# Attention softmax of a decoder layer: diagonal steps of 384 columns, mask and maximum in one instruction, key sums as products with a column of ones

## The chip, the cores and the metric

The kernel runs on one NeuronCore of a Trainium2 chip. The metric is the time of one execution in device microseconds; before the change the median of three runs is 2763.43 us (2759.95 to 2764.75). Engines are named as in the profile: PE is TensorE (PEld its weight loads), DVE is VectorE, ACT is ScalarE, POOL is GpSimd, SP is SyncE.

## The reference

One layer of a decoder over 2048 tokens of width 1024, all in float32. A normalised input is projected into three groups of columns: latent attention (8 heads, 96 wide for scores and 64 for values, causal), a spatial gating branch and a short convolution. Their outputs are normalised, joined and projected back, and a SwiGLU channel mixer with 2816 hidden columns follows. The change lies in the attention alone:

```
sc = (q_nope @ k_nope.T + q_rope @ k_rope.T) * scale
sc = where(kpos <= qpos, sc, lowest)
p  = softmax(sc, axis=-1)
out = p @ v
```

## The kernel before, in words

Products that need float32 accuracy are made of three products of float32r parts: each operand is split into a high part (ACT copies it) and a low part (DVE or POOL subtracts), and high x high, high x low and low x high are added in PSUM (`mm3_steps`, L204 to L206). A few small products take float32 operands as they are: `fold` (L518) is one.

The work goes in stages: input projections (to about 330 us), then attention woven with the rest of gating and the convolution (`weave`, L966; called from L1284 on), with the output projection of the first half, and with the channel mixer of the first half; from about 1800 us on the second half runs without attention. `attention` is a generator that yields an estimated cost after each piece, and the weaving takes so much of the other work for it. A scheduler of the build then sets each engine's order.

Attention has 64 units: 8 heads x 8 query blocks of 256 queries (`qp` 0 to 7; query blocks 0 to 3 of all heads come first). A unit has `qp + 1` steps, each over 256 keys, two blocks of 128 (`u`). The last step, `j2 == qp`, is the diagonal one: its second key block is seen by the second half of the queries alone. In all there are 288 steps, 64 of them diagonal.

For a unit, in the order in which it is planned:
- `row_max` (L420 to L440): for each half `e` of the queries, one product with queries on the partitions gives up to 512 scores in a PSUM bank `s`; DVE adds the mask `causal` to the last 128 columns of the last block (L435) and takes the maximum of each block (L436); with more than one block a last reduction (L439) joins them, negated, in column 96 of a tile `nmw`.
- `put_rows` (L442): PE transposes the two `nmw` tiles (128 x 97) into `mrow`, and ACT copies row 96 to the query tile as its 97th row, so that the scores come out with the maximum subtracted.
- `scores` (L451): per step two `mm3` into `sT` (keys on the partitions, 2 x 256 query columns). On a diagonal step DVE adds `causT` to two squares of 128 columns, the third square of `p` is set to zero by DVE (L467), and ACT takes the exponential in two pieces (L468, L469); otherwise one piece of 512 (L471). ACT copies `p` to `ph`, POOL (or DVE) makes `pl`. DVE adds every `p` to a running sum `acc` (L481, L484).
- `values` (L487), three steps later: per key block two products of the values with `ph` and `pl` into the PSUM bank `o`, of which there is one. At the unit's end DVE adds the halves of `acc` into `tot` (L503), ACT copies `o` to `os` (L505).
- `finish` (L510): PE transposes `tot` (two products, L516) and multiplies `os` by `fold` (two float32 products, L518), all into the bank `of`; DVE reduces the transposed `tot` to one sum per query (L520), takes the reciprocal and scales the output (L526).

The PSUM banks of `s`, `mrow` and `of` come from two tags of one bank each ("nx"), which the transposes of the output projection use too.

Of the kernel before, what the change touches and what calls it, by code (L numbers as in the profile page):

```python
# [11 lines left out]
F32 = mybir.dt.float32  # L12
# [3 lines left out]
AF = mybir.ActivationFunctionType  # L16
ALU = mybir.AluOpType
AX = mybir.AxisListType

P = 128  # L20
# [5 lines left out]
GT = 256  # L26
GELU_C = 0.044715
PB = 3
LAG = 3
TB = 3  # L30
# [6 lines left out]
NMB = 4  # L37
# [37 lines left out]
NEG = -1e30  # L75
# [9 lines left out]
def trunk(  # L85
# [6 lines left out]
    nc = tc.nc  # L92
# [7 lines left out]
    const = ctx.enter_context(tc.tile_pool(name="const", bufs=1))  # L100
# [12 lines left out]
    ident = const.tile([P, P], F32, name="ident")  # L113
# [4 lines left out]
    fold = const.tile([P, 64], F32, name="fold")  # L118
    for i in range(2):
        half = slice(64 * i, 64 * i + 64)  # L120
        nc.vector.tensor_copy(fold[half], ident[half, half])

    causal = const.tile([P, P], F32, name="causal")
    make_causal_mask(nc, causal, mask_val=NEG)
    causT = const.tile([P, P], F32, name="causT")
    nc.gpsimd.memset(causT, 0.0)
    nc.gpsimd.affine_select(out=causT, in_=causT, compare_op=ALU.is_ge, fill=NEG, base=0,
                            pattern=[[1, P]], channel_multiplier=-1)
    nmw = [const.tile([P, 97], F32, name=f"nmw{i}") for i in range(2 * NMB)]
    for t in nmw:  # L130
        nc.gpsimd.memset(t, 0.0)

    gp = const.tile([P, KD], F32, name="gp")

# [27 lines left out]
    def rows(t):  # L162
        return slice(t * P, (t + 1) * P)
# [215 lines left out]
    def attention(pools):  # L379
# [38 lines left out]
        mxs = {}  # L418

        def row_max(n, e, b):  # L420

            part, hd, qp = units[n]
            nk = (2 * qp + e + 1) * P
            nb = (nk + 511) // 512
            nm = nmw[(2 * n + e) % (2 * NMB)]
            if b == 0:
                mxs[n, e] = sp.tile([P, 4], F32, name="mx", bufs=4)
            mx = mxs[n, e]
            w = min(512, nk - 512 * b)
            wm = (w + GT - 1) // GT * GT  # L430
            s = bank("nx", "s")
            nc.tensor.matmul(s[:, :wm], qts[n][0:96, 0, rows(e)], kts[part, hd, b][0:96, 0:wm // GT, 0, :],  # L432
                             start=True, stop=True)
            if b == nb - 1:
                nc.vector.tensor_tensor(s[:, w - P:w], s[:, w - P:w], causal, op=ALU.add)  # L435
            nc.vector.tensor_reduce(mx[:, b:b + 1] if nb > 1 else nm[:, 96:97], s[:, :w],  # L436
                                    axis=AX.X, op=ALU.max, negate=nb == 1)
            if nb > 1 and b == nb - 1:
                nc.vector.tensor_reduce(nm[:, 96:97], mx[:, :nb], axis=AX.X, op=ALU.max, negate=True)  # L439
            return 0.7  # L440

        def put_rows(n):  # L442

            qt = qts[n]
            mrow = bank("nx", "mrow")
            for e in range(2):
                nc.tensor.transpose(mrow[0:97, rows(e)], nmw[(2 * n + e) % (2 * NMB)], ident)
            nc.scalar.activation(qt[96:97, 0, :], mrow[96:97, 0:GT], AF.Copy)
            return 0.4

        def scores(n, j2, st):  # L451
            part, hd, qp = units[n]
            qt = qts[n]
            s = bank("s", "sT")
            for u in range(2):
                j = 2 * j2 + u
                g, keys = j % 4 // 2, rows(j % 2)
                kt = kts[part, hd, j // 4]
                seen = slice(P if j2 == qp and u else 0, GT)
                mm3(s[:, u * 256 + seen.start:u * 256 + 256],  # L460
                    lambda k: kt[:, g, 0, keys], lambda k: kt[:, g, 1, keys],
                    lambda k: qt[:, 0, seen], lambda k: qt[:, 1, seen], 1)
            p = sp.tile([P, 512], F32, name="p", bufs=PB)
            if j2 == qp:
                for cs in (slice(0, P), slice(3 * P, 4 * P)):
                    nc.vector.tensor_tensor(s[:, cs], s[:, cs], causT, op=ALU.add)
                nc.vector.memset(p[:, 2 * P:3 * P], 0.0)  # L467
                nc.scalar.activation(p[:, 0:2 * P], s[:, 0:2 * P], AF.Exp)  # L468
                nc.scalar.activation(p[:, 3 * P:], s[:, 3 * P:], AF.Exp)  # L469
            else:  # L470
                nc.scalar.activation(p, s, AF.Exp)  # L471
            ph_ = sp.tile([P, 512], F32R, name="ph", bufs=PB)
            nc.scalar.activation(ph_, p, AF.Copy)  # L473
            pl_ = sp.tile([P, 512], F32R, name="pl", bufs=PB)
            eng = nc.vector if (n * 7 + j2) % 8 < lo_share[0] else nc.gpsimd
            eng.tensor_tensor(pl_, p, ph_.bitcast(F32), op=ALU.subtract)  # L476
            if j2 == 0:
                st["acc"] = p
            elif j2 == 1:
                acc = sp.tile([P, 512], F32, name="acc")  # L480
                nc.vector.tensor_tensor(acc, st["acc"], p, op=ALU.add)  # L481
                st["acc"] = acc
            else:
                nc.vector.tensor_tensor(st["acc"], st["acc"], p, op=ALU.add)  # L484
            return ph_, pl_

        def values(n, j2, pp, st):  # L487
            part, hd, qp = units[n]
            if j2 == 0:
                st["o"] = bank("o", "o")  # L490
            o = st["o"]
            for u in range(2):
                j = 2 * j2 + u
                at = P if j2 == qp and u else 0
                for i in range(2):
                    nc.tensor.matmul(o[:, at:256], vts[part, hd, j // 8][:, j % 8, :],  # L496
                                     pp[i][:, u * 256 + at:u * 256 + 256],
                                     start=j == 0 and i == 0, stop=j2 == qp and u == 1 and i == 1)
            if j2 < qp:
                return  # L500
            acc = st["acc"]
            tot = sp.tile([P, 256], F32, name="tot", bufs=TB)
            nc.vector.tensor_tensor(tot, acc[:, 0:256], acc[:, 256:512], op=ALU.add)  # L503
            os = sp.tile([P, 256], F32, name="os", bufs=TB)
            nc.scalar.activation(os, o[:, 0:256], AF.Copy)  # L505
            done[n] = tot, os

        done, yas = {}, {}

        def finish(n):  # L510

            _, hd, qp = units[n]
            of = bank("nx", "of")
            tot, os = done.pop(n)
# [11 lines left out]
            nc.vector.tensor_tensor(ya[:, :, 64 * (hd % 2):64 * (hd % 2) + 64],  # L526
                                    of[:, 256:384].rearrange("p (e d) -> p e d", e=2),
                                    rs[:, 2:4].unsqueeze(2).broadcast_to([P, 2, 64]), op=ALU.mult)
# [10 lines left out]
        for n in reversed(range(NU)):  # L539
            part, hd, qp = units[n]  # L540
# [47 lines left out]
        sp = pools[0]  # L588
# [5 lines left out]
        k = 0  # L594
        for n in range(NU):
            st = {}
            qp = units[n][2]
# [16 lines left out]
    with ExitStack() as ph:  # L614
# [3 lines left out]
        sp = ph.enter_context(tc.tile_pool(name="a_s", bufs=2, reuse_waits="tile"))  # L618
# [761 lines left out]
```

## Time and profile before

| | |
|---|---|
| median of three runs | 2763.43 us (2759.95 to 2764.75) |
| the profiled execution | 2758.1 us, of which the span (first to last instruction) is 2756.2 us |
| PE busy | 2673.9 us, 97% of the span, 14076 instructions |
| PEld busy | 2295.6 us, 83% |
| DVE busy | 1593.9 us, 58% |
| ACT busy | 1030.3 us, 37% |
| POOL busy | 751.9 us, 27% |
| mean granted TensorE clock | 0.979 |

The time of the profiled execution is that of the run in which the trace was taken; the span is what its rows cover. Busy times of one engine are unions over its instructions; matmuls are pipelined, so the duration of one is longer than its distance from the next, and it is the distances that add up to the time.

### The profile page before, as it was taken

What the parts mean: (1) busy time and instruction counts of PE and PEld (TensorE: products, weight loads), DVE (VectorE), ACT (ScalarE), POOL (GpSimd) and SP (SyncE); (2) the same over time, 40 slices, a digit from 0 to 9 for tenths busy, and PEclk for the clock granted to TensorE, in tenths of its full rate; (3) what the DMA queues carried; (4) which work ended last, traced back from release to release, by engine and by line L of the source; (5) the groups of instructions that cost most, each with busy time, mean ns of one, the idle gap of its engine ahead of it and who ended that gap; (6) DMA issues with size and microseconds to landing.
All of it is one profiled execution on the core that took longest, in us unless ns stands there. A gap on an engine that the chain in (4) does not pass through costs nothing. (4 is left out here: it accounts for less than half of the span.)

```text
span 2756.2 us, 37469 instructions
## 1 busy us (share of the span) xinstructions
PE 2673.9 (97%) x14076; PEld 2295.6 (83%) x14076; DVE 1593.9 (58%) x2805; ACT 1030.3 (37%) x1921; POOL 751.9 (27%) x835
## 2 busy tenths in 40 slices
PE   8999989998998999999999999999999999999998
PEld 7999878888787888888888888877878888888886
DVE  6555585657777666757687676755443333333335
ACT  6434353444455434444444444433531111111112
POOL 1222335765343332333343223313100000000004
PEclk9999988998999999999999999999999999999999
DMA  8755765454245333333252322254541111111113
GB/s 299 224 183 175 236 192 160 138 162 145 84 145 188 94 103 92 95 92 104 87 177 90 113 71 86 66 182 138 181 147 46 46 46 46 46 46 46 47 39 122
DMA packets 268945, 329.42 MB, mean 120 GB/s; under 512 B 17646, under 2 KB 198300, under 8 KB 264092
## 3 DMA queue, kind: packets, MB, share of 16 engines
q1 hardware_dynamic: 261244, 293.46, 34.0%
q0 software_dynamic: 5184, 29.36, 3.2%
q10 hardware_dynamic: 2336, 4.20, 0.4%
q8 instruction: 111, 1.82, 0.3%
q14 instruction: 70, 0.57, 0.1%
HBM read 238.56 MB, written 86.25 MB: 118 GB/s over the span
## 5 line engine op out<-in xcount | busy, mean ns | idle before, releaser
L476 POOL TENSOR_TENSOR pl<-p,ph 128x512 fp32r<-128x512 f32 x240 | 346.0, 1447 | 642.6 <-ACT ph L473 470.8
L1165 DVE TENSOR_TENSOR acc<-pd,acc 128x512 f32<-128x512 f32 x304 | 206.1, 688 | 225.1 <-PE pd L206 224.4
L204 PE MATMUL gu<-h2T,wgh 128*128 128x512 f32 x704 | 277.4, 394 | 2.6 <-ACT h2T L166 2.6
L205 PE MATMUL gu<-h2T,wgh 128*128 128x512 f32 x704 | 276.9, 393 | 0.0
L206 PE MATMUL gu<-h2T,wgl 128*128 128x512 f32 x704 | 276.8, 393 | 0.0
L204 PE MATMUL gu<-h2T,wuh 128*128 128x512 f32 x704 | 276.3, 392 | 0.0
L206 PE MATMUL gu<-h2T,wul 128*128 128x512 f32 x704 | 276.2, 392 | 0.0
L205 PE MATMUL gu<-h2T,wuh 128*128 128x512 f32 x704 | 275.9, 392 | 0.0
L204 PE MATMUL pd<-wd,gT 128*128 128x512 f32 x672 | 265.1, 395 | 2.3 <-ACT gT L166 1.6
L205 PE MATMUL pd<-wd,gT 128*128 128x512 f32 x672 | 262.7, 391 | 0.0
L206 PE MATMUL pd<-wd,gT 128*128 128x512 f32 x672 | 258.1, 393 | 0.0
L436 DVE TENSOR_REDUCE mx<-s 128x1 f32<-128x512 f32 (+3 forms) x288 | 175.6, 616 | 86.9 <-PE s L432 85.3
L473 ACT ACTIVATE ph<-p 128x512 fp32r<-128x512 f32 x288 | 180.3, 632 | 44.1 <-PE o L496 38.7
L1181 POOL DMA_DIRECT2D x<-x_d x8 | 4.7, 589 | 696.9 <-PE gu L206 691.7
L471 ACT ACTIVATE p<-sT 128x512 f32<-128x512 f32 x224 | 132.6, 594 | 144.8 <-PE sT L206 130.7
L484 DVE TENSOR_TENSOR acc<-acc,p 128x512 f32<-128x512 f32 x168 | 166.1, 988 | 22.2 <-ACT p L469 11.4
L204 PE MATMUL sT<-zone 97*128 97x256 f32 x576 | 167.6, 291 | 4.9 <-ACT p L471 4.0
L205 PE MATMUL sT<-zone 97*128 97x256 f32 x576 | 167.5, 291 | 0.0
L206 PE MATMUL sT<-zone 97*128 97x256 f32 x576 | 167.2, 290 | 0.0
L496 PE MATMUL o<-ph,zone 128*128 128x256 f32 x576 | 157.8, 292 | 5.1 <-ACT os L505 2.2
L204 PEld LDWEIGHTS gu<-h2T,wgh 128*128 128x128 f32 x704 | 132.5, 188 | 31.1 <-ACT h2T L166 3.2
L206 PEld LDWEIGHTS gu<-h2T,wgl 128*128 128x128 f32 x704 | 132.7, 188 | 29.4
(278 smaller groups left out, 6216.7 us busy)
## 6 DMA issues: line engine op xcount, KB each, us to landing
raw<-in_w_gate_dram SPq DMA_DIRECT2D x66, 512.0 KB
raw<-in_w_up_dram SPq DMA_DIRECT2D x66, 512.0 KB
raw_d<-in_w_down_dram SPq DMA_DIRECT2D x66, 512.0 KB
ht<-hT_d POOLq DMA_DIRECT2D x20, 1024.0 KB, 5.6
zone<-k_d SPq DMA_DIRECT2D x48, 384.0 KB
hT_d<-ht SPq DMA_DIRECT2D x16, 1024.0 KB
xt<-in_x_dram SPq DMA_DIRECT2D x31, 512.0 KB
zone<-v_d SPq DMA_DIRECT2D x24, 512.0 KB
```

What stands on the lines that cost most here:

```text
L204: nc.tensor.matmul(ps, ah(k), bh(k), start=k == 0, stop=False)
L205: nc.tensor.matmul(ps, ah(k), bl(k), start=False, stop=False)
L206: nc.tensor.matmul(ps, al(k), bh(k), start=False, stop=k == n - 1)
L436: nc.vector.tensor_reduce(mx[:, b:b + 1] if nb > 1 else nm[:, 96:97], s[:, :w], axis=AX.X, op=ALU.max, negate=nb == 1)
L471: nc.scalar.activation(p, s, AF.Exp)
L473: nc.scalar.activation(ph_, p, AF.Copy)
L476: eng.tensor_tensor(pl_, p, ph_.bitcast(F32), op=ALU.subtract)
L484: nc.vector.tensor_tensor(st["acc"], st["acc"], p, op=ALU.add)
L496: nc.tensor.matmul(o[:, at:256], vts[part, hd, j // 8][:, j % 8, :], pp[i][:, u * 256 + at:u * 256 + 256], start=j == 0 and i == 0, stop=j ...
L1165: nc.vector.tensor_tensor(acc[tt][:, cols], pd, acc[tt][:, cols], op=ALU.add)
L1181: nc.gpsimd.dma_start(x2, x2_d[t0 + tt])
```

## The change

The running sum on the diagonal step, its zeroed square, the halves' addition and the transposes of the sums go. Instead the unit's end multiplies pieces of `p` and `acc`, as stationary 128 x 128 operands, by a column of ones, and adds the results in columns 256 and 257 of the bank `o`; there the sums stand with the queries on the partitions, and ACT's copy takes them along. On a diagonal step the second key block's 128 columns are written right behind the first's 256, so that exponential, copy, subtraction and mask run over 384 columns. `causal` is 512 wide, zero ahead of the mask, so that DVE adds it and takes the maximum of a unit's last block in one instruction, which also starts from the other blocks' result. `nmw` is one tile with a column per unit half, so that `put_rows` transposes 128 x 1.

```
-    causal = const.tile([P, P], F32, name="causal")
-    make_causal_mask(nc, causal, mask_val=NEG)
+    causal = const.tile([P, 512], F32, name="causal")
+    nc.gpsimd.memset(causal[:, 0:512 - P], 0.0)
+    make_causal_mask(nc, causal[:, 512 - P:512], mask_val=NEG)
+    ones = const.tile([P, 1], F32, name="ones")
+    nc.vector.memset(ones, 1.0)
...
-    nmw = [const.tile([P, 97], F32, name=f"nmw{i}") for i in range(2 * NMB)]
-    for t in nmw:
-        nc.gpsimd.memset(t, 0.0)
+    nmw = const.tile([P, 2 * NMB], F32, name="nmw")
...
-            if b == nb - 1:
-                nc.vector.tensor_tensor(s[:, w - P:w], s[:, w - P:w], causal, op=ALU.add)
-            nc.vector.tensor_reduce(mx[:, b:b + 1] if nb > 1 else nm[:, 96:97], s[:, :w],
-                                    axis=AX.X, op=ALU.max, negate=nb == 1)
-            if nb > 1 and b == nb - 1:
-                nc.vector.tensor_reduce(nm[:, 96:97], mx[:, :nb], axis=AX.X, op=ALU.max, negate=True)
+            if b < nb - 1:
+                nc.vector.tensor_reduce(mx[:, b:b + 1], s[:, :w], axis=AX.X, op=ALU.max, negate=True)
+                return 0.7
+            if nb > 2:
+                nc.vector.tensor_reduce(mx[:, 3:4], mx[:, :nb - 1], axis=AX.X, op=ALU.min)
+            least = -NEG if nb == 1 else mx[:, 3:4] if nb > 2 else mx[:, 0:1]
+            nc.vector.tensor_tensor_reduce(s[:, :w], s[:, :w], causal[:, 512 - w:512], -1.0, least,
+                                           ALU.add, ALU.min, nm)
...
-                nc.tensor.transpose(mrow[0:97, rows(e)], nmw[(2 * n + e) % (2 * NMB)], ident)
-            nc.scalar.activation(qt[96:97, 0, :], mrow[96:97, 0:GT], AF.Copy)
+                i = (2 * n + e) % (2 * NMB)
+                nc.tensor.transpose(mrow[0:1, rows(e)], nmw[:, i:i + 1], ident)
+            nc.scalar.activation(qt[96:97, 0, :], mrow[0:1, 0:GT], AF.Copy)
...
-            p = sp.tile([P, 512], F32, name="p", bufs=PB)
+            p = sp.tile([P, 512], F32, name="p", bufs=PB + 1)
+            w = 3 * P if j2 == qp else 512
             if j2 == qp:
-                for cs in (slice(0, P), slice(3 * P, 4 * P)):
-                    nc.vector.tensor_tensor(s[:, cs], s[:, cs], causT, op=ALU.add)
-                nc.vector.memset(p[:, 2 * P:3 * P], 0.0)
-                nc.scalar.activation(p[:, 0:2 * P], s[:, 0:2 * P], AF.Exp)
-                nc.scalar.activation(p[:, 3 * P:], s[:, 3 * P:], AF.Exp)
-            else:
-                nc.scalar.activation(p, s, AF.Exp)
+                diag = s.rearrange("p (b k) -> p b k", k=P)[:, 0:4:2]
+                nc.vector.tensor_tensor(diag, diag, causT.unsqueeze(1).broadcast_to([P, 2, P]), op=ALU.add)
+            nc.scalar.activation(p[:, :w], s[:, :w], AF.Exp)
...
-            if j2 == 0:
+            if j2 == qp:
+                st["last"] = p
+            elif j2 == 0:
                 st["acc"] = p
...
-            acc = st["acc"]
-            tot = sp.tile([P, 256], F32, name="tot", bufs=TB)
-            nc.vector.tensor_tensor(tot, acc[:, 0:256], acc[:, 256:512], op=ALU.add)
-            os = sp.tile([P, 256], F32, name="os", bufs=TB)
-            nc.scalar.activation(os, o[:, 0:256], AF.Copy)
-            done[n] = tot, os
+            last = st["last"]
+            for e in range(2):
+                parts = [last[:, rows(b)] for b in ((0,), (1, 2))[e]]
+                if qp:
+                    parts += [st["acc"][:, rows(e)], st["acc"][:, rows(2 + e)]]
+                for i, part_ in enumerate(parts):
+                    nc.tensor.matmul(o[:, 256 + e:257 + e], part_, ones, start=i == 0, stop=i == len(parts) - 1)
+            os = sp.tile([P, 258], F32, name="os", bufs=TB)
+            nc.scalar.activation(os, o[:, 0:258], AF.Copy)
+            done[n] = os
...
-                nc.tensor.transpose(of[:, rows(e)], tot[:, rows(e)], ident)
-            for e in range(2):
-                nc.tensor.matmul(of[:, 256 + 64 * e:320 + 64 * e], os[:, rows(e)], fold, start=True, stop=True)
-            rs = sp.tile([P, 4], F32, name="rs")
-            nc.vector.tensor_reduce(rs[:, 0:2], of[:, 0:256].rearrange("p (e k) -> p e k", e=2),
-                                    axis=AX.X, op=ALU.add)
-            nc.vector.reciprocal(rs[:, 2:4], rs[:, 0:2])
+                nc.tensor.matmul(of[:, 64 * e:64 * e + 64], os[:, rows(e)], fold, start=True, stop=True)
+            rs = sp.tile([P, 2], F32, name="rs")
+            nc.vector.reciprocal(rs, os[:, 256:258])
```

Lines of the kernel after stand four to nine further down: L434 is the product of `row_max`, L442 the new instruction, L452 `put_rows`, L500 and L511 the products of `values`, L524 `fold`.

How it moves instructions, at two places. PE at the end of the last unit, woven with the channel mixer. Before, the last values into `o`, then the transposes of `tot`, then the mixer's second product (`pd`):

```order
L496 MATMUL o<-ph,zone 128x128
L496 MATMUL o<-pl,zone 128x128
L516 MATMUL of<-ident,tot 128x128 x2
L204 MATMUL pd<-wd_19006,gT 128x512
L205 MATMUL pd<-wd_19007,gT 128x512
```

The same place after, with the mixer's first product (`gu`) behind it:

```order
L205 MATMUL pd<-wd_18650,gT 128x512
L206 MATMUL pd<-wd_18651,gT 128x512
L207 MATMUL pd<-wd_18650,gT 128x512
L511 MATMUL o<-ones,p 128x1
L511 MATMUL o<-ones,acc 128x1 x2
L511 MATMUL o<-ones,p 128x1 x2
L511 MATMUL o<-ones,acc 128x1 x2
L205 MATMUL gu<-h2T_10074,wgh 128x512
```

Seven products with the column of ones stand where two transposes stood. Over the program PE has 416 of them (224 from `p`, 192 from `acc`), and 128 transposes of `tot` fewer; of the 128 transposes of `nmw`, 49 stand right behind another one (38 before).

DVE at the same unit's end. Before, from the zeroed square of the diagonal step to the scaled output (L1165 is the mixer's addition):

```order
L467 MEMSET p 128x128
L484 TENSOR_TENSOR acc<-acc,p 128x512
L466 TENSOR_TENSOR sT<-sT,causT 128x128 x2
L484 TENSOR_TENSOR acc<-acc,p 128x512
L1165 TENSOR_TENSOR acc_15535<-pd,acc_15535 128x512
L476 TENSOR_TENSOR pl<-p,ph 128x512
L503 TENSOR_TENSOR tot<-acc 128x256
L1165 TENSOR_TENSOR acc_15536<-pd,acc_15536 128x512 x2
L1165 TENSOR_TENSOR acc_15537<-pd,acc_15537 128x512 x2
L520 TENSOR_REDUCE rs<-of 128x2
L522 RECIPROCAL rs<-rs 128x2
L526 TENSOR_TENSOR ya_18173<-of,rs 128x2x64
```

And after:

```order
L488 TENSOR_TENSOR acc<-acc,p 128x512
L472 TENSOR_TENSOR sT<-sT,causT 128x2x128
L1169 TENSOR_TENSOR acc_15218<-pd,acc_15218 128x512
L478 TENSOR_TENSOR pl<-p,ph 128x384
L1169 TENSOR_TENSOR acc_15219<-pd,acc_15219 128x512 x2
L1169 TENSOR_TENSOR acc_15220<-pd,acc_15220 128x512 x2
L526 RECIPROCAL rs<-os 128x2
L530 TENSOR_TENSOR ya_17821<-of,rs 128x2x64
```

Zeroing, one of the two mask additions, the diagonal step's addition to `acc`, `tot` and the reduction are gone; nothing is added on DVE here.

## Rows read from the trace of the kernel before

**Rows 1.** The page: span, and busy time of each engine.

```profile
span 2756.2 us, 37469 instructions
PE 2673.9 (97%) x14076; PEld 2295.6 (83%) x14076; DVE 1593.9 (58%) x2805; ACT 1030.3 (37%) x1921; POOL 751.9 (27%) x835
```

**Rows 2.** Stretches: busy us of each engine, granted clock, DMA share, GB/s.

```profile
core 0: us, PE busy (x) PEld busy (x) DVE busy (x) ACT busy (x) POOL busy (x), PEclk, DMA share, GB/s
...
380.00:440.00 60.00, 50.85 (x232) 44.80 (x232) 43.28 (x114) 27.82 (x65) 29.39 (x32) 0.69 0.45 142
440.00:640.00 200.00, 197.25 (x1314) 179.93 (x1313) 121.29 (x281) 82.56 (x197) 141.18 (x169) 1.00 0.48 147
640.00:680.00 40.00, 34.25 (x194) 30.61 (x193) 34.26 (x75) 19.93 (x46) 23.22 (x22) 0.79 0.61 181
680.00:720.00 40.00, 33.98 (x187) 29.35 (x187) 31.79 (x77) 22.88 (x50) 16.56 (x15) 0.80 0.38 119
...
870.00:890.00 20.00, 14.26 (x66) 11.75 (x66) 17.79 (x21) 14.22 (x24) 6.98 (x5) 0.66 0.71 238
890.00:1390.00 500.00, 499.69 (x2705) 431.62 (x2706) 335.91 (x564) 210.99 (x345) 157.60 (x94) 1.00 0.33 98
...
1410.00:1810.00 400.00, 399.57 (x2165) 345.25 (x2164) 279.39 (x447) 170.54 (x286) 138.84 (x89) 1.00 0.32 101
```

**Rows 3.** PE and PEld by line and form: count, busy us, mean ns.

```profile
L518 PE MATMUL of<-fold,os 128*128 128x64 f32 x256 | 37.7, 271 | 0.0
...
L516 PE MATMUL of<-ident,tot 128*128 128x128 f32 x128 | 26.5, 287 | 3.1 <-DVE mx L436 2.2 <-ACT zone L448 0.4 <-DVE ya L526 0.3
```

**Rows 4.** PEld in order of time (start us, us, what), full clock.

```profile
920.62 0.37 PEld L516 LDWEIGHTS of<-ident,tot 128*128 128x128 f32 x2
920.96 0.52 PEld L518 LDWEIGHTS of<-fold,os 128*128 128x128 f32 x4
921.40 0.19 PEld L432 LDWEIGHTS s<-zone 96*128 96x128 f32 x1
921.52 0.19 PEld L206 LDWEIGHTS pd<-wd,gT 128*128 128x128 f32 x1
921.75 0.19 PEld L205 LDWEIGHTS pd<-wd,gT 128*128 128x128 f32 x1
```

**Rows 5.** PEld in order of time around two transposes of `nmw`.

```profile
1386.07 0.40 PEld L447 LDWEIGHTS mrow<-ident,nmw 128*97 128x97 f32 x2
1386.41 0.19 PEld L206 LDWEIGHTS gu<-h2T,wul 128*128 128x128 f32 x1
1386.52 0.19 PEld L204 LDWEIGHTS gu<-h2T,wuh 128*128 128x128 f32 x1
```

**Rows 6.** DVE by line and form, the forms that the change touches.

```profile
L484 DVE TENSOR_TENSOR acc<-acc,p 128x512 f32<-128x512 f32 x168 | 166.1, 988 | 22.2 <-ACT p L469 11.4 <-ACT p L471 9.4
...
L503 DVE TENSOR_TENSOR tot<-acc 128x256 f32<-128x256 f32 x56 | 49.8, 889 | 2.8 <-PE of L516 2.2
L466 DVE TENSOR_TENSOR sT<-sT,causT 128x128 f32<-128x128 f32 x128 | 37.2, 291 | 15.6 <-PE sT L206 14.7
L435 DVE TENSOR_TENSOR s<-s,causal 128x128 f32<-128x128 f32 x128 | 36.9, 292 | 49.1 <-PE s L432 48.5
L520 DVE TENSOR_REDUCE rs<-of 128x2 f32<-128x256 f32 x64 | 26.7, 417 | 32.9 <-PE of L518 32.9
L467 DVE MEMSET p<- 128x128 f32 x64 | 10.5, 165 | 6.1 <-POOL pl L476 6.0
```

**Rows 7.** Who PEld waited for in 640 to 720 us: us, times, longest.

```profile
PEld s L432 <- ACT zone L448: 2.5, 4, 1.0
PEld o L496 <- ACT ph L473: 2.1, 2, 1.3
```

**Rows 8.** PEld in order of time, the same loads at the lower clock.

```profile
392.50 0.88 PEld L518 LDWEIGHTS of<-fold,os 128*128 128x128 f32 x4
393.30 0.19 PEld L204 LDWEIGHTS sT<-zone 97*128 97x128 f32 x1
```

More of the change, by code (lines that the diff above doesn't have):

```diff
@@ L424, in row_max @@
             nb = (nk + 511) // 512
-            nm = nmw[(2 * n + e) % (2 * NMB)]
-            if b == 0:
+            i = (2 * n + e) % (2 * NMB)
+            nm = nmw[:, i:i + 1]
+            if b == 0 and nb > 1:
                 mxs[n, e] = sp.tile([P, 4], F32, name="mx", bufs=4)
-            mx = mxs[n, e]
+            mx = mxs.get((n, e))
             w = min(512, nk - 512 * b)
@@ L446, in put_rows @@
             for e in range(2):
-                nc.tensor.transpose(mrow[0:97, rows(e)], nmw[(2 * n + e) % (2 * NMB)], ident)
-            nc.scalar.activation(qt[96:97, 0, :], mrow[96:97, 0:GT], AF.Copy)
+                i = (2 * n + e) % (2 * NMB)
+                nc.tensor.transpose(mrow[0:1, rows(e)], nmw[:, i:i + 1], ident)
+            nc.scalar.activation(qt[96:97, 0, :], mrow[0:1, 0:GT], AF.Copy)
             return 0.4
@@ L459, in scores @@
                 seen = slice(P if j2 == qp and u else 0, GT)
-                mm3(s[:, u * 256 + seen.start:u * 256 + 256],
+                mm3(s[:, u * 256:u * 256 + GT - seen.start],
                     lambda k: kt[:, g, 0, keys], lambda k: kt[:, g, 1, keys],
                     lambda k: qt[:, 0, seen], lambda k: qt[:, 1, seen], 1)
-            p = sp.tile([P, 512], F32, name="p", bufs=PB)
+            p = sp.tile([P, 512], F32, name="p", bufs=PB + 1)
+            w = 3 * P if j2 == qp else 512
             if j2 == qp:
-                for cs in (slice(0, P), slice(3 * P, 4 * P)):
-                    nc.vector.tensor_tensor(s[:, cs], s[:, cs], causT, op=ALU.add)
-                nc.vector.memset(p[:, 2 * P:3 * P], 0.0)
-                nc.scalar.activation(p[:, 0:2 * P], s[:, 0:2 * P], AF.Exp)
-                nc.scalar.activation(p[:, 3 * P:], s[:, 3 * P:], AF.Exp)
-            else:
-                nc.scalar.activation(p, s, AF.Exp)
+                diag = s.rearrange("p (b k) -> p b k", k=P)[:, 0:4:2]
+                nc.vector.tensor_tensor(diag, diag, causT.unsqueeze(1).broadcast_to([P, 2, P]), op=ALU.add)
+            nc.scalar.activation(p[:, :w], s[:, :w], AF.Exp)
             ph_ = sp.tile([P, 512], F32R, name="ph", bufs=PB)
-            nc.scalar.activation(ph_, p, AF.Copy)
+            nc.scalar.activation(ph_[:, :w], p[:, :w], AF.Copy)
             pl_ = sp.tile([P, 512], F32R, name="pl", bufs=PB)
             eng = nc.vector if (n * 7 + j2) % 8 < lo_share[0] else nc.gpsimd
-            eng.tensor_tensor(pl_, p, ph_.bitcast(F32), op=ALU.subtract)
-            if j2 == 0:
+            eng.tensor_tensor(pl_[:, :w], p[:, :w], ph_[:, :w].bitcast(F32), op=ALU.subtract)
+            if j2 == qp:
+                st["last"] = p
+            elif j2 == 0:
                 st["acc"] = p
@@ L496, in values @@
                     nc.tensor.matmul(o[:, at:256], vts[part, hd, j // 8][:, j % 8, :],
-                                     pp[i][:, u * 256 + at:u * 256 + 256],
+                                     pp[i][:, u * 256:u * 256 + 256 - at],
                                      start=j == 0 and i == 0, stop=j2 == qp and u == 1 and i == 1)
@@ L513, in finish @@
             of = bank("nx", "of")
-            tot, os = done.pop(n)
+            os = done.pop(n)
             for e in range(2):
-                nc.tensor.transpose(of[:, rows(e)], tot[:, rows(e)], ident)
-            for e in range(2):
-                nc.tensor.matmul(of[:, 256 + 64 * e:320 + 64 * e], os[:, rows(e)], fold, start=True, stop=True)
-            rs = sp.tile([P, 4], F32, name="rs")
-            nc.vector.tensor_reduce(rs[:, 0:2], of[:, 0:256].rearrange("p (e k) -> p e k", e=2),
-                                    axis=AX.X, op=ALU.add)
-            nc.vector.reciprocal(rs[:, 2:4], rs[:, 0:2])
+                nc.tensor.matmul(of[:, 64 * e:64 * e + 64], os[:, rows(e)], fold, start=True, stop=True)
+            rs = sp.tile([P, 2], F32, name="rs")
+            nc.vector.reciprocal(rs, os[:, 256:258])
             if hd % 2 == 0:
@@ L526, in finish @@
             nc.vector.tensor_tensor(ya[:, :, 64 * (hd % 2):64 * (hd % 2) + 64],
-                                    of[:, 256:384].rearrange("p (e d) -> p e d", e=2),
-                                    rs[:, 2:4].unsqueeze(2).broadcast_to([P, 2, 64]), op=ALU.mult)
+                                    of[:, 0:128].rearrange("p (e d) -> p e d", e=2),
+                                    rs.unsqueeze(2).broadcast_to([P, 2, 64]), op=ALU.mult)
             if hd % 2 == 1:
```

## The prediction

> **What bounds the kernel now.** I read the page's busy times first. PE is busy for 97% of the span, DVE for 58%, ACT for 37%, POOL for 27% [rows 1]. A busy PE need not be PE at its peak, so the second view is that of stretches: whether PE also had the full granted clock and no gaps in the stage that changes. Attention runs from about 340 to 1810 us. From 890 to 1390 and from 1410 to 1810 us PE is busy for 499.69 of 500 and 399.57 of 400 us at clock 1.00 [rows 2]: there DVE's time, 336 of 500 us, is hidden, and any work taken from DVE is worth nothing, while any work put on PE is paid in full. The exceptions are four short stretches, 380 to 440, 640 to 680, 680 to 720 and 870 to 890 us, in which PE is idle for 9.2, 5.8, 6.0 and 5.7 us and the mean clock is 0.69, 0.79, 0.80 and 0.66 (a mix of 1.2 and 2.4 GHz), while DVE is busy for 72 to 89% [rows 2]. Lost there, against a busy PE at full clock: 26.7 us idle, and by the clock 60 x 0.31 + 40 x 0.21 + 40 x 0.20 + 20 x 0.34 = 41.8 us, together 68.5 us. That is all that a lighter DVE could give back in the stages that the change touches, apart from some microseconds scattered elsewhere.
>
> The third view is PE's own instructions, to price one. What counts is not the duration of a product (271 ns for `fold`'s [rows 3]) but its distance from the next. `fold` has 128 products in the program and 256 in the trace [rows 3]: a product of two float32 operands is issued as two, each with its own load of weights. The transposes of `tot` are 128 in both.
>
> **The products with a column of ones** are the largest term. 64 units x 3, and 4 more in each of the 56 units whose query block is not the first, make 192 + 224 = 416 products, float32 by float32, so 832 loads of a 128 x 128 stationary operand, each followed by a product that streams one column. The nearest row is `fold`: the same kind of operand, loaded the same way, streaming 64 columns. Four such loads begin at 920.96 and the next instruction's load at 921.40 us [rows 4]: 0.11 us each. Next to them loads behind products of 512 columns stand 0.23 us apart [rows 4], so between long products a load is hidden and between short ones it is the load that sets the pace; whether 64 columns or one are streamed behind it should not matter. The load behind the last short product is not hidden either, whereas the first one is, so each costs its 0.11 us wherever it stands: 832 x 0.11 = 91.5 us. PE is the full engine, so all of it lies on the path.
>
> Here a rule of the Trainium skill gives another price. Its page "TensorE: Matmul & The Clock Gate", section "Back-to-back issue gap", gives a product of 1 to 64 columns about 60 cycles, that is some 25 ns at full clock; by it the 832 would cost an estimated 21 us. The rows of `fold` are four times that, and the same page's section on LDWEIGHTS says why: a load takes a time that goes by its columns, 128 here. I go by the rows; the cheap price is the first rival below.
>
> **What goes from PE.** 128 transposes of `tot`: their two loads begin at 920.62, the next at 920.96 us, of which the first waits behind a long product [rows 4]; I take 0.11 us each, 14.1 us off. The transposes of `nmw` load one column instead of 97. A single one between long products gains nothing, since its load is hidden and the next product's load behind it still takes its time: after the second of the pair the loads follow in 0.11 us [rows 5]. Only where a transpose stands right behind another, 49 times in the changed order, may the second's load vanish: between 0 and 49 x 0.11 = 5.4 us. I take 2, as the 128 columns must still stream. Scores and values on the diagonal are the same products at other places in the bank: 0.
>
> **What goes from DVE, and what it is worth.** 56 additions to `acc` at 0.988 (55.3 us), `tot` (49.8), the reduction of sums (26.7), the zeroing (10.5), the mask on the row scores (36.9) and, two squares in one instruction at the 417 ns of a reduction over as many columns of PSUM, 64 x 0.417 = 26.7 instead of 37.2 (10.5) [rows 6]: 190 us. Against it stands the new instruction. No row shows it; it replaces a reduction over the same columns, and I bound what it costs beyond that by 0 and by the 292 ns of the mask addition that it takes in, 128 x 0.292 = 37 us. The nearer row is 0 extra, since an addition and a reduction go over the columns once each and this one goes once. So DVE loses 150 to 190 us, about 3 us per unit. ACT and POOL lose a quarter of their 512 columns on 64 steps. All of this is hidden behind PE except in the four stretches. There, PE waits for ACT's copy of the row maximum and for exponentials [rows 7]: chains through several engines, of which DVE is one link. So a lighter DVE shortens these waits without abolishing them, and fewer gaps may also keep the clock up. The bounds are 0 and 68.5 us. I take 18 us, about a quarter: the releasers named are ACT more than DVE, and the added loads fall into the same stretches (32 units lie in the 340 us from 380 to 720, so some 13 of them with 169 loads in these 140 us), where the clock halves their pace: four `fold` loads took from 392.50 to 393.30, 0.20 us each [rows 8].
>
> **New waits.** The bank `o` is held until the products with ones are done; they stand on PE itself, so nothing waits that would not wait in PE's order anyway, and ACT's copy of `o` stays as long. `p` of the last step is kept some steps longer, with one more buffer; the running sum's buffer waits for PE instead of DVE. I cost these at 0: the cover is the other work in PE's order, and if it failed, an exponential would be late by one run of ones, 14 x 0.11 = 1.5 us, at few units.
>
> **The sum.** +91.5 - 14.1 - 2 - 18 = +57 us on the profiled execution's 2758.1 us (span 2756.2 us and 1.9 around it): 2815.5 us. The median of the runs shown stands 5.3 us above that execution; with it the sum is 2821. I forecast 2818 us, in between.
>
> **The rivals.**
>
> *The loads hide* (ends faster). If weights could be loaded two ahead, under products of 512 columns that leave 0.12 us of room each, the ones would cost little more than their own single column. For it: most of the units are woven with such products. Against it: `fold` stands among the same 512-column products and still takes 0.11 us per load [rows 4]. At 0 to 0.02 us each, some 8 us, the sum is 8 - 14 - 2 - 18 = -26 us on the profiled execution, on the median about 2738. It decides if a load costs under (14 + 2 + 18) / 832 = 0.04 us. Chance 0.05.
>
> *The clock falls* (ends slower still). A run of seven products with ones is 1.5 us in which PE streams 14 columns. Where such runs meet gaps, the granted clock may fall to 1.2 GHz as it did in the four stretches, and then every product behind them takes twice as long. For it: the falls are in the stages with many short products and gaps. Against it: 440 to 640 us has many short products too, and stays at 1.00 [rows 2]. If half of the 832 loads ran at 0.20 us (37 us more) and the gain in the four stretches did not come (18), the time is about 2818 + 55 = 2873. Chance 0.11.
>
> *DVE's relief reaches all of the four stretches.* If they all ran like 890 to 1390 us, 68.5 us came back: +91.5 - 14.1 - 2 - 68.5 = +7 us, 2765 to 2770 us. For it: DVE is busy for 72 to 89% there. Against it: the releasers are mostly others [rows 7]. Chance 0.06.
>
> The change does what it says: the products, their number and their places stand in the order of its instructions, so I give no chance to the opposite.
>
> **How the numbers follow.** The forecast gets 0.78. Its own range: 40 us of the four stretches given back and 5 by the transposes, on the profiled execution 2758.1 + 91.5 - 14.1 - 5 - 40 = 2790; nothing given back, on the median, and 15 us for 169 loads at the lower clock: 2763.4 + 77.4 + 15 = 2856. To hold 8 in 10 I widen it a little into the neighbours, 2786 to 2858: that leaves out the first rival (0.05), most of the second (about 0.09) and most of the third (0.05). About 0.2%, 5.5 us, is what a measurement of this kernel can tell from no change. Faster by more than that: the first rival, 0.05. Within it: the lower part of the third, 0.05. Slower: 0.90.
>
> **What would show it.** PE's instructions up by 832 - 128 = 704, to 14780. The loads of the ones about 0.11 us apart, in runs of up to 14. DVE's busy time down by 150 to 190 us with nothing to show for it between 890 and 1810 us of the old time, where the same work should end later by some 0.11 x 13 = 1.4 us for each unit in it. Low-clock time in the first half of attention no more than before. The forecast is wrong if the loads of the ones stand closer than 0.11 us, if the stretches with a low clock vanish or spread, or if the new DVE instruction takes well over a microsecond for 512 columns, so that the row maxima come late.

## The result and the profile after

The changed kernel takes 2807.97 us (median of four runs, 2805.22 to 2813.49), the kernel before, over the runs made beside it, 2761.69 us. The ratio is 1.0172 with a 95% interval of 1.0155 to 1.0190: slower by 46 us, where 2818 us and a range of 2786 to 2858 were forecast.

The page of the kernel after: span and busy time of each engine, against [rows 1].

```profile
span 2806.5 us, 38424 instructions
PE 2737.8 (98%) x14780; PEld 2361.0 (84%) x14780; DVE 1437.5 (51%) x2462; ACT 1021.5 (36%) x1857; POOL 730.1 (26%) x828
```

PE has exactly the 704 instructions more that were forecast and stays the full engine; DVE is 156 us lighter, within the 150 to 190 us forecast, and the kernel is slower all the same. The time went into the attention stage alone. From the first product of `row_max` to the last scaled output it took 328 to 1799 us before and takes 328 to 1850 us after, 51 us more, and what follows is as long as it was. Groups of PE and PEld, and the order of PEld's loads in one unit, late in that stage:

```profile
L511 PE MATMUL o<-ones,p 128*128 128x1 f32 x448 | 65.8, 249 | 0.0
L511 PEld LDWEIGHTS o<-ones,p 128*128 128x128 f32 x448 | 63.4, 201 | 0.7
L511 PEld LDWEIGHTS o<-ones,acc 128*128 128x128 f32 x384 | 54.3, 200 | 0.7
...
L452 PEld LDWEIGHTS mrow<-ident,nmw 128*1 128x1 f32 x128 | 9.9, 85 | 8.2 <-DVE mx L437 2.0 <-DVE nmw L442 2.0 <-issue 1.1
```

```profile
1816.40 0.19 PEld L500 LDWEIGHTS o<-pl,zone 128*128 128x128 f32 x1
1816.51 0.30 PEld L511 LDWEIGHTS o<-ones,p 128*128 128x128 f32 x2
1816.73 0.53 PEld L511 LDWEIGHTS o<-ones,acc 128*128 128x128 f32 x4
1817.17 0.53 PEld L511 LDWEIGHTS o<-ones,p 128*128 128x128 f32 x4
1817.62 0.53 PEld L511 LDWEIGHTS o<-ones,acc 128*128 128x128 f32 x4
1818.07 0.19 PEld L205 LDWEIGHTS gu<-h2T,wuh 128*128 128x128 f32 x1
```

448 + 384 = 832 loads, and fourteen of them between 1816.51 and 1818.07 us: 0.111 us each, as for `fold` before [rows 4], though each is followed by a product of a single column.

To see where a kernel's time goes I use three numbers of the attention stage in its profiled execution: its length, PE's idle time in it (neither a product nor a load runs) and the low clock, that is the time that the trace's clock records show at 1.2 instead of 2.4 GHz (half of it is lost). Length less idle less half the low clock is PE's work at full clock.

| | stage, us | idle PE | low clock | PE's work at full clock | median, all |
|---|---|---|---|---|---|
| before | 1470.6 | 44.2 | 92.2 | 1380.3 | 2762 |
| after | 1521.5 | 31.1 | 78.5 | 1451.2 | 2808 |

So +70.8 us of work on PE, and 13.1 us of idle time and 6.9 us of clock given back: +50.8, against a span longer by 50.3 us. Low clock that falls on idle time loses nothing; that is 9 us in either row, so both figures of work are some 5 us too low and their difference stands.

### The profile page after: what moved, and what is told of

It reads as the page before. It is cut to its first block, busy times and chain, and to the rows that moved or that the text cites. A ratio compares the mean times of both kernels' runs of the same rounds, so it can differ in the third digit from the quotient of the medians.

```text
span 2806.5 us, 38424 instructions
## 1 busy us (share of the span) xinstructions
PE 2737.8 (98%) x14780; PEld 2361.0 (84%) x14780; DVE 1437.5 (51%) x2462; ACT 1021.5 (36%) x1857; POOL 730.1 (26%) x828
## 5 line engine op out<-in xcount | busy, mean ns | idle before, releaser
L478 POOL TENSOR_TENSOR pl<-p,ph 128x512 fp32r<-128x512 f32 (+1 forms) x240 | 327.9, 1371 | 673.8 <-ACT ph L475 535.8
L473 ACT ACTIVATE p<-sT 128x512 f32<-128x512 f32 (+1 forms) x288 | 163.1, 569 | 215.6 <-PE sT L207 135.7
L475 ACT ACTIVATE ph<-p 128x512 fp32r<-128x512 f32 (+1 forms) x288 | 173.9, 607 | 80.6 <-PE o L500 69.6
L437 DVE TENSOR_REDUCE mx<-s 128x1 f32<-128x512 f32 x192 | 130.6, 685 | 107.0 <-PE s L434 106.3
L205 PE MATMUL sT<-zone 97*128 97x256 f32 x576 | 165.3, 287 | 1.3 <-ACT p L473 1.2
L206 PE MATMUL sT<-zone 97*128 97x256 f32 x576 | 164.4, 285 | 0.0
L207 PE MATMUL sT<-zone 97*128 97x256 f32 x576 | 164.1, 285 | 0.0
L500 PE MATMUL o<-ph,zone 128*128 128x256 f32 x576 | 154.8, 288 | 6.5 <-ACT os L513 6.5
L500 PE MATMUL o<-pl,zone 128*128 128x256 f32 x576 | 153.6, 292 | 7.1 <-POOL pl L478 6.9
L205 PEld LDWEIGHTS gu<-h2T,wgh 128*128 128x128 f32 x704 | 132.7, 189 | 31.1 <-ACT h2T L167 2.7
```

What stands on the lines that cost most here:

```text
L437: nc.vector.tensor_reduce(mx[:, b:b + 1], s[:, :w], axis=AX.X, op=ALU.max, negate=True)
L473: nc.scalar.activation(p[:, :w], s[:, :w], AF.Exp)
L475: nc.scalar.activation(ph_[:, :w], p[:, :w], AF.Copy)
L478: eng.tensor_tensor(pl_[:, :w], p[:, :w], ph_[:, :w].bitcast(F32), op=ALU.subtract)
```

## The experiments

All medians stand beside runs of the kernel before on the same chip (2761 to 2763 us).

**Each half of the change by itself.** First the change without its products with ones (the diagonal squares are stored so that one addition of 384 columns keeps the sum in `acc`):

```
-                for i, part_ in enumerate(parts):
-                    nc.tensor.matmul(o[:, 256 + e:257 + e], part_, ones, start=i == 0, stop=i == len(parts) - 1)
...
+            if qp:
+                nc.vector.tensor_tensor(tot, acc[:, 0:256], acc[:, 256:512], op=ALU.add)
...
+                nc.tensor.transpose(of[:, rows(e)], tot[:, rows(e)], ident)
```

> The change without its products with ones: the sums over the keys are made as before (acc, tot, two transposes), on the 384 columns of a diagonal step; mask and maximum in one instruction and the one-column transposes stay. If the loads of the ones are what costs (704 loads net, 0.11 us each, 78 us), PE is back at 14076 instructions and the time at 2740 to 2762 us, the gain against the kernel before being what a lighter DVE gives back. If another part of the change costs the time (the new DVE instruction, the layout, the transposes), it stays above 2785 us.

Measured: 2755.13 us, ratio 0.9978 (0.9968 to 0.9989), PE back at 14076 instructions. All of the change but the ones is worth 3 to 9 us, and without them it beats both kernels. Its stage takes 1460.9 us, with 64.9 us of low clock instead of the 92.2 before: the gain lies in the clock.

Then the kernel before with the ones alone (the third square of a diagonal step is no longer zeroed, since nothing reads it, and its copy and its subtraction go in two pieces):

```
-            tot = sp.tile([P, 256], F32, name="tot", bufs=TB)
-            nc.vector.tensor_tensor(tot, acc[:, 0:256], acc[:, 256:512], op=ALU.add)
...
+                parts = [last[:, rows(b)] for b in ((0,), (1, 3))[e]]
+                if qp:
+                    parts += [st["acc"][:, rows(e)], st["acc"][:, rows(2 + e)]]
+                for i, part_ in enumerate(parts):
+                    nc.tensor.matmul(o[:, 256 + e:257 + e], part_, ones, start=i == 0, stop=i == len(parts) - 1)
```

> The kernel before with the products with ones alone (sums over the keys as in the change; mask, maximum, layout and transposes as before). If the loads of the ones are what costs, PE has 14780 instructions and the time is 2805 to 2825 us, as the change or somewhat more, since less is taken from DVE. If another part costs it, within 10 us of 2762.

Measured: 2804.63 us, ratio 1.0160 (1.0143 to 1.0176), just under the range given and within 4 us of the whole change. In the profiled execution the stage takes 1525.4 us, 54.8 more than before and 3.9 more than after the whole change; the part behind the stage is some 10 us shorter than in either, which does not go with the ones (end of this section). The ones are the loss, all of it.

**More loads, and what is streamed behind them.**

```
                 for i, part_ in enumerate(parts):
                     nc.tensor.matmul(o[:, 256 + e:257 + e], part_, ones, start=i == 0, stop=i == len(parts) - 1)
+                for i, part_ in enumerate(parts):
+                    nc.tensor.matmul(o[:, 258 + e:259 + e], part_, ones, start=i == 0, stop=i == len(parts) - 1)
```

> The change with every product with ones issued a second time, into two columns that nobody uses: 832 more loads, nothing else. If each load costs its 0.11 us on a PE without slack, 2808 + 91 = 2899 us, 2885 to 2910. If loads hide under other products, or if the gaps take them up, under 2850. If runs of them draw the clock down, over 2920, with low clock between 900 and 1800 us.

Measured: 2974.71 us, ratio 1.0781: 167 us for 832 loads, where 91 were expected; the third case came true. The stage's idle time went down to 25.0 us, but its low clock rose from 78.5 to 245.8 us, also where the kernel after has almost none. Stretches from 900 us on of this kernel (busy us of each engine, granted clock, DMA share, GB/s), one of the kernel after, and the doubled kernel's loads in order of time at one place:

```profile
900.00:1200.00 300.00, 293.45 (x1614) 256.23 (x1614) 175.05 (x257) 124.75 (x204) 86.34 (x63) 0.94 0.38 113
1200.00:1500.00 300.00, 300.00 (x1680) 262.10 (x1679) 163.51 (x266) 114.20 (x182) 79.92 (x51) 0.97 0.29 86
1500.00:1800.00 300.00, 297.34 (x1619) 258.92 (x1619) 179.46 (x272) 117.02 (x192) 93.37 (x66) 0.95 0.34 103
```

```profile
1500.00:1800.00 300.00, 300.00 (x1674) 260.72 (x1673) 178.35 (x279) 119.67 (x190) 91.47 (x56) 1.00 0.28 83
```

```profile
976.30 0.55 PEld L511 LDWEIGHTS o<-ones,p 128*128 128x128 f32 x2
976.73 0.97 PEld L511 LDWEIGHTS o<-ones,acc 128*128 128x128 f32 x4
977.58 0.55 PEld L513 LDWEIGHTS o<-ones,p 128*128 128x128 f32 x2
978.01 0.97 PEld L513 LDWEIGHTS o<-ones,acc 128*128 128x128 f32 x4
```

Between 1200 and 1500 us PE is busy for all of 300 us, and the clock is 0.97 all the same. The clock records show 43 falls to 1.2 GHz in this stage; 33 of them come without idle time just before, each behind a run of these products. Where the clock is low the loads are 0.21 us apart, (977.58 - 976.73) / 4. PE's work at full clock is 1536.1 us, 85.0 more than after: 0.102 us per load. Another 84 us are clock, half of 245.8 - 78.5; 6 us of idle time went.

Sixty-four equal columns of ones instead of one:

```
-    ones = const.tile([P, 1], F32, name="ones")
+    ones = const.tile([P, 64], F32, name="ones")
...
-                    nc.tensor.matmul(o[:, 256 + e:257 + e], part_, ones, start=i == 0, stop=i == len(parts) - 1)
+                    nc.tensor.matmul(o[:, 256 + 64 * e:320 + 64 * e], part_, ones, start=i == 0, stop=i == len(parts) - 1)
...
```

> The change with 64 columns of ones instead of one. If the load sets the pace, as with fold, nothing changes: 2803 to 2815 us. If a product of one column is cheaper than one of 64, 832 more stretches of 63 columns show: 2825 us or more.

Measured: 2791.07 us, ratio 1.0107 (1.0089 to 1.0125): 17 us *faster* than one column, which neither theory had. Only 7.5 us of it lie in the attention stage (1514.0 against 1521.5 us); 11 lie behind it, where there are no ones (end of this section). In the stage PE's work is the same (1453.6 against 1451.2 us), so the load does set the pace; low clock fell from 78.5 to 51.2 us. Over the four executions of each the mean granted clock is 0.985 to 0.989, against 0.979 to 0.985. That and the doubled run suggested one cause: runs of products of one column bring the low clock. Its test is the doubled run with 64 columns (the edits of the last two together):

> Every product with ones issued twice, as in the run that took 2975 us, but with 64 columns of ones instead of one. If the loads cost 0.10 to 0.11 us each whatever is streamed, and the rest of that run's time was low clock that runs of one-column products bring, the time is 2791 + 85 to 92, about 2880 us (2865 to 2895), with the low clock of the attention stage well under the 246 us seen there. If the second 832 loads cost twice the first for another reason, it stays above 2940 us.

Measured: 2872.49 us, ratio 1.0397, inside the range, and 102 us less than with one column, 90 of them in the stage. The same stretches:

```profile
900.00:1200.00 300.00, 293.42 (x1642) 256.17 (x1641) 183.28 (x274) 126.95 (x200) 89.08 (x60) 0.97 0.36 107
1200.00:1500.00 300.00, 299.08 (x1727) 261.95 (x1726) 173.61 (x278) 120.76 (x196) 88.84 (x64) 1.00 0.32 94
1500.00:1800.00 300.00, 298.40 (x1688) 261.22 (x1688) 180.53 (x277) 117.76 (x187) 88.41 (x57) 0.99 0.32 95
```

Low clock in the stage: 54.6 us instead of 245.8, and none of its falls (5 here, 8 in the run before) comes without idle time of PE just ahead of it. PE's work at full clock rose from 1453.6 to 1543.7 us: 0.108 us per load. With 128 columns (`ones` and the slices widened again):

> The change with 128 columns of ones. If a load of 0.11 us hides the streaming, and more streamed columns keep the clock up, 2775 to 2795 us with at most the 51 us of low clock that 64 columns left in the attention stage. If 128 columns of float32 take longer than the load, the 832 products show it: 2805 us or more.

Measured: 2788.16 us, ratio 1.0091, low clock 41.0 us, PE's work 1455.2: float32 products of 128 columns still hide behind their loads, but for some 4 us in 832.

**Fewer loads.** DVE adds the halves of `acc`, five products per unit instead of seven:

```
+            if qp:
+                tot = sp.tile([P, 256], F32, name="tot", bufs=2)
+                nc.vector.tensor_tensor(tot, st["acc"][:, 0:256], st["acc"][:, 256:512], op=ALU.add)
...
-                    parts += [st["acc"][:, rows(e)], st["acc"][:, rows(2 + e)]]
+                    parts += [tot[:, rows(e)]]
```

> The change, but DVE first adds the two halves of acc (56 additions of 256 columns, 0.9 us each, 50 us of DVE), so that a unit has five products with ones instead of seven: 224 loads fewer. If loads on PE are the price and DVE is hidden, 2808 - 24.6 = 2783 us, 2775 to 2792. If the relief of DVE is what matters, 2808 us or more.

Measured: 2786.49 us, ratio 1.0085: 21.5 us less for 224 loads (22.6 in the stage), while DVE does more.

The products in float32r, where one load does for a product:

```
-                    nc.tensor.matmul(o[:, 256 + e:257 + e], part_, ones, start=i == 0, stop=i == len(parts) - 1)
+                    nc.tensor.matmul(o[:, 256 + 2 * e:258 + 2 * e], part_, onesr, start=i == 0, stop=i == len(parts) - 1)
```

> The change with the products with ones in float32r: acc is kept rounded to float32r and the last step's piece is the high part ph, so that the sums are of rounded values (the low parts are left out); two equal columns of ones. 416 products stay, each with one load instead of two. If loads are the price, 2808 - 46 = 2762 us, 2750 to 2772. If products are, whatever their loads, 2800 us or more.

Measured: 2749.97 us, ratio 0.9955 (0.9940 to 0.9970): 58 us less for 416 loads, at the edge of the range, but only 47.6 of it in the stage. PE's work fell by 40.4 us (0.097 per load), the low clock from 78.5 to 58.0 us. Then both together:

> The products with ones in float32r on rounded sums, and the halves of acc added on DVE first: 304 products with one load each instead of 832 loads (sums of rounded values, low parts left out). If loads are the price, 112 fewer than the 416 of the float32r run take off 11 us: 2750 - 11 = 2739 us (2733 to 2747), under both kernels. If the float32r run's remaining time is not in the loads, 2748 us or more.

Measured: 2750.46 us, ratio 0.9964: nothing gained, a miss. And with 64 columns of ones, which had helped above (the sums on both sides of the values in the bank, since a wider copy of `o` left no room in SBUF):

> The 304 float32r products on halved sums (values rounded, low parts left out), with 64 columns of ones instead of two, the sums on both sides of the values in the bank so that ACT copies 258 columns. The two-column run had 85 us of low clock in the attention stage, against 51 us with 64 columns of float32. If the streamed columns hold the clock, low clock falls to 60 us or less and the time from 2750 to 2730 to 2742 us; if that run's low clock comes from the gaps alone, nothing changes: 2746 us or more.

Measured: 2760.67 us, ratio 0.9991: a miss again, low clock 78.5 us; its extra 10 us lie behind the stage. In these three kernels PE's work is 1410.8, 1393.3 and 1397.8 us, and the stage is 1474 us long in each: what is taken from PE comes back as idle time (34.1, 37.9, 36.6) and low clock (58.0, 85.3, 78.5). Other waits seem to set the time here; which, no run shows.

**Is DVE's relief worth anything?** Needless additions on DVE, four per unit:

```
+            for _ in range(4):
+                nc.vector.tensor_tensor(heavy, heavy, heavy, op=ALU.add)
```

> The change with four needless DVE additions of 384 columns at each unit's end, on a tile of zeros: about 3 us per unit, 190 us, what the change took from DVE. If the part of the loads that did not show in the time (78 us priced, 46 measured) came from DVE's relief, the time rises by 20 to 35 us to 2828 to 2843. If DVE is hidden and the relief was worth nothing, 2803 to 2815.

Measured: 2818.49 us, ratio 1.0205, but inconclusive: depending on nothing, all were placed ahead of attention. Stretches before the stage and in it:

```profile
0.00:344.00 344.00, 315.24 (x2008) 292.91 (x2008) 318.11 (x741) 154.20 (x363) 113.21 (x203) 0.98 0.67 209
...
344.00:1864.00 1520.00, 1490.79 (x8682) 1311.49 (x8683) 858.38 (x1497) 644.55 (x1147) 564.72 (x513) 0.97 0.38 116
```

DVE is busy for 318 of the first 344 us, and the stage starts 16 us late, with the same 858 us of DVE as after (861). The second try ties them to the unit:

```
+                nc.vector.tensor_tensor(heavy, heavy, last[:, 0:384], op=ALU.add)
```

> Needless DVE additions again, four of 384 columns per unit, but each reads the unit's last piece of p, so that they cannot run ahead of the attention stage: 256 of 0.6 us or more, 150 us or more of DVE between 380 and 1850 us, where the first try had none. If the part of the loads that did not show in the time came from DVE's relief, the attention stage grows by 10 to 20 us (idle PE and low clock back towards the 44 and 92 us of the kernel before) and the time is 2818 us or more. If it came from PE's own loads filling the waits, idle PE and low clock stay near 31 and 79 us and the time within 2800 to 2814.

Measured: 2820.14 us, ratio 1.0215 (1.0196 to 1.0234), 12 us over the change. DVE, by line and by stretch:

```profile
L515 DVE TENSOR_TENSOR heavy<-heavy,p 128x384 f32<-128x384 f32 x256 | 199.8, 781 | 13.1 <-ACT p L475 10.0
```

```profile
328.00:1850.00 1522.00, 1489.08 (x8659) 1308.56 (x8658) 1038.10 (x1763) 645.37 (x1148) 581.57 (x512) 0.97 0.39 117
```

200 us of DVE, more than the change took from it, lengthen the profiled stage by 6.6 us: idle 32.8 us instead of 31.1, low clock 81.9 instead of 78.5. The time favours the first theory, idle time and clock the second; between them the relief is worth 7 to 12 us, if adding DVE work at this place undoes what the change took elsewhere.

**All kernels side by side**, each from its profiled execution (us; the last column is the time from the end of the attention stage to the end of the program):

| kernel | loads of ones | stage | idle PE | low clock | PE's work | behind the stage |
|---|---|---|---|---|---|---|
| before | 0 | 1470.6 | 44.2 | 92.2 | 1380.3 | 957.6 |
| change without the ones | 0 | 1460.9 | 46.6 | 64.9 | 1381.9 | 960.5 |
| float32r, halves | 304 | 1473.9 | 37.9 | 85.3 | 1393.3 | 947.7 |
| the same, 64 columns | 304 | 1473.7 | 36.6 | 78.5 | 1397.8 | 957.4 |
| float32r | 416 | 1473.9 | 34.1 | 58.0 | 1410.8 | 947.6 |
| halves | 608 | 1498.9 | 31.9 | 71.7 | 1431.2 | 959.7 |
| after | 832 | 1521.5 | 31.1 | 78.5 | 1451.2 | 956.8 |
| ones alone | 832 | 1525.4 | 29.7 | 85.3 | 1453.0 | 947.5 |
| 64 columns | 832 | 1514.0 | 34.8 | 51.2 | 1453.6 | 945.7 |
| 128 columns | 832 | 1509.1 | 33.4 | 41.0 | 1455.2 | 948.2 |
| doubled | 1664 | 1684.0 | 25.0 | 245.8 | 1536.1 | 955.8 |
| doubled, 64 columns | 1664 | 1594.2 | 23.2 | 54.6 | 1543.7 | 947.8 |

The last column falls into two groups, some 947 and 957 us, and neither the ones nor their columns sort them. There is no attention there. The same stretch of the kernel after, and of that with 64 columns:

```profile
2150.00:2650.00 500.00, 500.00 (x2168) 406.27 (x2167) 176.53 (x227) 84.17 (x108) 0.00 (x0) 1.00 0.16 50
```

```profile
2150.00:2650.00 500.00, 500.00 (x2197) 412.33 (x2196) 179.51 (x232) 82.09 (x106) 0.00 (x0) 1.00 0.16 49
```

PE is busy throughout at full clock in both and gets through 2168 products in one and 2197 in the other. What sets this pace no run shows. Before and after stand in the same group, so their difference is free of it; of differences between groups, some 10 us of the medians are not the experiment's.

## Why the prediction was right

**PE is the bound, and DVE is hidden.** Right, but for a rest: 704 instructions more on PE and 156 us less of DVE made the kernel slower, and 200 us of DVE put back cost 7 to 12 us.

**The price of a load.** Right: 0.111 us apart in the run above, and over whole kernels 0.102 to 0.108 us (doubled), 0.097 (float32r). Net of the transposes I priced 77.4 us; PE's work rose by 70.8. The first rival, loads that hide, fell with that. That it is the load with its columns that takes the time, and not any pair of load and product, the transposes of `nmw` show where one stands behind a run of ones. PEld in the kernel after, where it loads one column, and in that with the ones alone, where it loads 97:

```profile
1059.45 0.53 PEld L511 LDWEIGHTS o<-ones,acc 128*128 128x128 f32 x4
1059.89 0.09 PEld L452 LDWEIGHTS mrow<-ident,nmw 128*1 128x1 f32 x1
1059.92 0.19 PEld L205 LDWEIGHTS sT<-zone 97*128 97x128 f32 x1
```

```profile
1065.12 0.41 PEld L512 LDWEIGHTS o<-ones,acc 128*128 128x128 f32 x3
1065.45 0.17 PEld L449 LDWEIGHTS mrow<-ident,nmw 128*97 128x97 f32 x1
1065.54 0.19 PEld L206 LDWEIGHTS sT<-zone 97*128 97x128 f32 x1
```

The next load begins 0.03 us after a load of one column, 0.09 after one of 97, 0.11 after one of 128.

The cheap price that I set aside, 25 ns from the page "TensorE: Matmul & The Clock Gate" of the Trainium skill (its section "Back-to-back issue gap"), would have made an estimated 21 us of the 832. The same page's section "LDWEIGHTS (loading the stationary operand)" gives the columns divided by 1.2 as a load's ns, an estimated 107 ns for 128 columns, and the 0.097 to 0.111 us of the runs agree with that.

**The transposes of `nmw`.** I took 2 us; the trace shows none. Products in order of time:

```profile
1028.04 0.38 PE L452 MATMUL mrow<-ident,nmw 128*1 128x128 f32 x2
1028.26 0.50 PE L511 MATMUL o<-ones,acc 128*128 128x1 f32 x4
```

Two of them still take 0.22 us. It is not their loads, behind which the next load can follow in 0.03 us (above); that it is the 128 columns that they stream is likely, but was not tested. The kernel without the ones has these transposes too, and its PE's work is 1381.9 us against 1380.3 before: nothing gained there either.

**The four stretches.** 18 us were forecast to come back, and 13.1 + 6.9 = 20 did, over the whole stage. The size was right, and in part by luck: its reason, a lighter DVE, explains only a part. (The bound of 68.5 us was some 4 too high, since low clock while PE is idle was counted twice; and units of the first half hold 12 loads, so 13 of them 156 and not 169.) The kernel without ones has 55 us less of busy DVE in the stage than the kernel before, and its idle PE is 46.6 us against 44.2; what it gains is low clock. Idle PE goes with the loads instead: 37 us at 304, 31.1 at 832, 25.0 at 1664. So part of the added work simply stands in PE's waits, and a wait that it fills costs nothing. How much of the 20 us is which, the runs don't settle.

**New waits at 0.** Wrong: one was there. Stretch of the kernel after, and ACT and PE in it:

```profile
692.50:698.50 6.00, 0.14 (x2) 0.00 (x0) 0.85 (x2) 0.93 (x3) 0.30 (x1) 0.63 1.07 307
698.50:711.00 12.50, 12.47 (x58) 12.18 (x58) 4.97 (x14) 5.72 (x11) 4.10 (x4) 0.50 0.42 124
```

```profile
690.81 0.63 ACT L475 ACTIVATE ph<-p 128x512 fp32r<-128x512 f32 x1 [0.50 <-PE o L500]
697.57 0.63 ACT L167 ACTIVATE wo<-raw 128x512 fp32r<-128x512 f32 x1 [6.13 <-DMA raw<-in_w_out_dram]
698.10 0.37 ACT L513 ACTIVATE os<-o 128x258 f32<-128x258 f32 x1
```

```profile
698.52 0.58 PE L500 MATMUL o<-ph,zone 128*128 128x256 f32 x1 [5.89 <-ACT os L513]
```

ACT waits 6.13 us for a piece of the output weights; the copy of `o` is queued behind it, and PE, which needs the one bank `o`, is idle from 692.6 to 698.5, after which the clock is 0.50 until 711. About 12 us at one place (5.9 idle, and half of the 12.5 that follow); the releaser named is a DMA, not DVE. Between 600 and 780 us ACT's longest wait for such a piece is 1.7 us in the kernel before and 2.3 without the ones, and 4.0 to 6.4 in every kernel with them; why, no run shows. Idle time fell all the same, since other waits went. Such a wait is one reason why the third rival, all of the four stretches given back, did not come.

**The clock.** The second rival had the mechanism, runs of one-column products, but its size was too large for this change: it took low clock to rise, and it fell, 92.2 to 78.5 us (mean granted clock 0.975 to 0.982 over 57 executions before, 0.979 to 0.985 over four after). That it is there all the same the 64 columns show: 27 us of low clock, about 14 us of time, are owed to the single column; idle time and work take some 6 of the 14 back. At twice the loads it decides, with 84 us.

**The forecast of 2818 against 2808.** On the profiled execution +57 were forecast and +50 measured; 7 of it is the price of a load, the rest cancels.

## What to carry to other kernels

On a full PE, price a small product by the weights that it loads: loading 128 stationary columns costs 0.10 to 0.11 us here with 1, 64 or 128 columns behind them, and a float32 product, which loads twice, twice that. Work taken from an engine that hides behind PE is worth next to nothing; moving it to PE costs in full, save what falls into PE's waits. Where short products of one column must come in runs on a full PE, try equal extra columns as long as the load hides them: 64 instead of one took 7.5 us off the attention stage here and 90 us off that with twice as many; with 304 float32r products it took nothing off. And compare stages before medians: kernels here differ by 10 us in a part that no experiment touched.

## What the runs showed that was not expected

A busy PE can lose its clock: with 26 one-column loads per unit on average the stage spends 245.8 of 1684 us at 1.2 GHz, with the same loads and 64 columns 54.6 of 1594. And in the three float32r kernels the stage does not get shorter with PE's work: they differ by 13 us of it or more, and it takes 1474 us in each; the kernel without ones, with 11 us less of work than the least of them, takes 1460.9.
